# Halves of w_in and w_out stored to scratch in the second sub-block and loaded from there in the third and fourth

## The chip, the cores and the metric

The kernel runs on one core of one Trainium2 chip. The metric is the device time of one execution in microseconds (us), the median of several runs. The profile is one further execution, taken by the hardware profiler; its times count from the first instruction of the program.

## The reference

One inference step of one decoder layer. 2048 prompt tokens of one request and 32 decoding tokens (8 requests of 4) with 1024 features go through three sub-layers, each behind an RMS norm and with a residual add:

```
q, k, v, r, a, u, sv = split(rmsnorm(x) @ w_in)             # 256 256 512 512 16 512 512
o     = gated_linear_attention(q / 8, k, v, log_sigmoid(a @ w_alpha + b_alpha) / 16)
o     = rmsnorm(o) * silu(r)
s_out = gelu(u) * (tril(w_s) @ rmsnorm(gelu(sv)) + b_s)     # inside chunks of 128 tokens
h = x + concat(o, s_out) @ w_out                            # the mixer
h = h + softmax(rmsnorm(h) @ wq_x @ mk^T / 16) @ mv @ wo_x  # 256 memory tokens, 4 heads
h = h + (gelu(conv3(rmsnorm(h) @ w_gate)) * (rmsnorm(h) @ w_up)) @ w_down   # 2816 wide
y = rmsnorm(h)
```

w_in is 1024 x 2576, w_out 1024 x 1024; both are used for every token. Everything is fp32. Outputs are y for prompt and decoding tokens, the attention and convolution states, memory keys and values, and the decoding tokens' sv.

## The kernel before, in words

**Sub-blocks.** The prompt is cut into four sub-blocks of 512 tokens (s = 0 to 3), worked through one after the other: mixer, attention over the memory, feed-forward. The 32 decoding tokens ride along in the mixer of the second sub-block (`SAMPLE_MIX = 1`) and in the feed-forward of the third (`SAMPLE_FFN = 2`); their attention over their own caches is done beside the second sub-block's feed-forward. By the trace, the mixers' projections begin at about 73, 805, 1580 and 2250 us.

**Three products for one.** To keep fp32 precision, an operand is split into two parts of a faster type: `hi`, a rounded copy made by ACT (line 84), and `lo`, the rest, subtracted by DVE or POOL (line 85). `mm3` (lines 92 to 94) then multiplies hi by hi, hi by lo and lo by hi.

**Units of weights.** Weights come in units of 128 partitions by 1024 floats. `wload` (line 99) loads one on SP's queue into one of five raw buffers (`wraw`, names r_...), `wsplit` (line 105) splits it into one of five `whi` and one of five `wlo` buffers (h_..., l_...); `wunit` (line 112) does both. `wready` (line 118) instead loads two halves that already lie in DRAM scratch straight into a `whi` and a `wlo` buffer, with two loads on SP (line 124); the attention and the feed-forward from the second sub-block on work like that. `wkeep` (line 129) is `wunit` followed at once by two stores of the halves to scratch on SP (line 134); the first sub-block uses it for w_down. The other weights of the feed-forward are stored there too in the first sub-block, as parts and sums for a product scheme of seven instead of eight (lines 163 to 179), and the folded attention matrices are stored by `put` and `flush` (lines 288 to 294).

**Steps.** The program is a list of steps; a step has a function and the units that it needs. `run` (line 475) goes through the list in order and keeps the units `AHEAD = 5` in front of the steps:

```
for i, st in enumerate(steps):
    now[0] = i
    flush(i - 1)
    need += sum(cost(u) for u in st.units)
    while at < len(queue) and made < need + AHEAD:
        j, u = queue[at]
        ready.setdefault(j, []).append(u() if callable(u) else wunit(*u))
        made += cost(u)
        at += 1
    st.fn(*ready.pop(i, []))
```

`put` only notes a store together with the number of the step; `flush` issues it on ACT's queue once the program is two steps further, so that nothing waits on a fresh result. `weave` (line 457) mixes side steps into the main ones by their numbers. The framework sets all waits and, when the kernel is built, the order of the instructions on every engine from a simulated schedule; each engine and each queue then works in that fixed order, so a queue whose next transfer must wait holds up those behind it.

**The mixer.** `proj_steps` (line 780) makes 20 units of w_in per sub-block: `tm_steps` (line 677) for sv, v and r with tokens on the partitions, four units each, and `fm_step` (line 660) for k, q and two halves of u with features on the partitions, two units each. The 16 columns of a are held in SBUF throughout. `out_proj_steps` (line 1142) takes 8 units of w_out, first the four of the gating half, then the four of the attention half. Between them are woven the gated linear attention (`gla_steps`, line 892: seven levels of masked products, states and decay on DVE, ACT and POOL), the spatial gating (`sgu_steps`, whose `mix` makes z and its halves ch and cl), and the final norm and output of the sub-block before (`final_steps`, line 1566). All 28 units pass through `wunit` in each of the four sub-blocks. In the second, `smp` inside `gla_steps` loads the states of the decoding requests (sg, line 1068, on SP).

**The way into a sub-block.** `norm_in_steps` (line 697) loads x in four pieces of 128 tokens through four buffers on SP (line 708): two pieces first, two (`second`) once the first have been transposed, and, in the second sub-block, the decoding tokens. Then come the norm's statistics, a broadcast (bcp_x) and the split xh, xl, which the projection ws (sv) needs first. These steps are woven into the last w_down steps of the sub-block before (line 1654).

Of the kernel before, what the change touches and what calls it, by code (L numbers as in the profile page):

```python
# [9 lines left out]
F32 = mybir.dt.float32  # L10
F32R = mybir.dt.float32r
U8 = mybir.dt.uint8
AF = mybir.ActivationFunctionType
# [14 lines left out]
SAMPLE_MIX = 1  # L28
# [5 lines left out]
Q0, K0, V0, R0, A0, U0, SV0 = 0, 256, 512, 1024, 1536, 1552, 2064  # L34
# [3 lines left out]
def hymba_step_kernel(  # L38
# [9 lines left out]
    nc = tc.nc  # L48
    act, dve, pool, pe = nc.scalar, nc.vector, nc.gpsimd, nc.tensor
# [7 lines left out]
    dp = ctx.enter_context(tc.tile_pool(name="dp", bufs=1, space=DRAM))  # L57
# [54 lines left out]
    def wunit(*spec):  # L112
        return wsplit(wload(*spec), spec[-1])
# [4 lines left out]
    def wready(src, name):  # L118

        def load():  # L120
            out = []
            for x, tag in enumerate(("whi", "wlo")):
                t = wp.tile(list(src.shape[0:1]) + list(src.shape[2:]), F32R, tag=tag, name=f"{tag}_{name}")
                nc.sync.dma_start(t.bitcast(F32), src[:, x])
                out.append(t)
            return tuple(out)
        return load

    def wkeep(dst, *spec):

        def load():
            out = wunit(*spec)
            for x, t in enumerate(out):
                nc.sync.dma_start(dst[:, x], t.bitcast(F32))
            return out
        return load

# [147 lines left out]

    late, now = [], [0]

    def put(dst, src):
        late.append((now[0], dst, src))

    def flush(before=None):
        while late and (before is None or late[0][0] < before):
            _, dst, src = late.pop(0)
            nc.scalar.dma_start(dst, src)

    def rstd_of(out, ss, p, n, inv):
        t = narrow("rt")
# [51 lines left out]
    for l in range(7):  # L349
# [3 lines left out]
        v = mf[:, :64].rearrange("p (n h) -> p n h", h=half)  # L353
# [295 lines left out]
    def chunks_of(sample):  # L649
        return [(0, 272), (272, 272)] if sample else [(0, 512)]  # L650
# [6 lines left out]
            return hi, lo  # L657
        return load

    def fm_step(w, m0, get_xs, sample, evac, name, make=None):  # L660
# [12 lines left out]
        if make is not None:  # L673
            return Step(fn, [wmake(w, 4 * j, 4, m0, 256, f"{name}{j}", make, j) for j in range(2)])
        return Step(fn, [(w, 4 * j, 4, m0, 256, f"{name}{j}") for j in range(2)])

    def tm_steps(w, m0, get_xs, sample, evac, name):

        ps = {}

        def fn(j, wu):
            xs = get_xs()
            wh, wl = wu
            for c in range(5 if sample else 4):
                n = 128 if c < 4 else NS
                cs = slice(c * 128, c * 128 + n)
                if j == 0:
                    ps[c] = acc(f"t_{name}{c}") if c < 4 else mps(f"t_{name}{c}")
                for kk in range(2):
                    k = 2 * j + kk  # L690
                    mm3(ps[c][:n], xs[k][0][:, cs], xs[k][1][:, cs], wh[:, kk], wl[:, kk], k == 0, k == 7)
                if j == 3:
                    evac(ps[c][:n], c, n)
        return [Step(lambda wu, j=j: fn(j, wu), [(w, 2 * j, 2, m0, 512, f"{name}{j}")]) for j in range(4)]


    def norm_in_steps(B):
# [82 lines left out]
    def proj_steps(B):  # L780
        s, sample = B.s, B.mix_sample
        T = TM if sample else SB
        nt = 5 if sample else 4
        w = w_in[0]
        xs = lambda: B.xs

        def ev_tm(key, f):
            def evac(ps, c, n):
                if c == 0:
                    B.__dict__[key] = [U(f"{key}{s}{c}") for c in range(nt)]  # L790
                f(B.__dict__[key][c][:n, :512], ps)
# [23 lines left out]
        out = tm_steps(w, SV0, xs, sample, ev_tm("sv", gelu), f"ws{s}")  # L815
        out.append(Step(a_fn))
        out.append(fm_step(w, K0, xs, sample, ev_fm("k", 0, cpy), f"wk{s}"))
        out.append(fm_step(w, Q0, xs, sample,
                           ev_fm("q", 0, lambda o, i: act.activation(o, i, AF.Copy, scale=0.125)), f"wq{s}"))
        out += tm_steps(w, V0, xs, sample, ev_tm("v", cpy), f"wv{s}")  # L820
        out += [fm_step(w, U0 + h * 128, xs, sample, ev_fm("u", h, gelu), f"wu{s}{h}") for h in (0, 2)]
        out += tm_steps(w, R0, xs, sample, ev_tm("r", cpy), f"wr{s}")
        return out

    def norm_of(src, ss, c, n):
# [61 lines left out]
    for p in range(2):  # L887
        t = cp.tile([128, 128], F32, tag=f"S{p}", name=f"Sz{p}", bufs=2)
# [721 lines left out]
    for s in range(NSB):  # L1610
        B = NS_()
# [8 lines left out]
    after = []  # L1620
    for s, B in enumerate(blocks):
        proj = proj_steps(B)
        gla, gtail = gla_steps(B)
        sgu_st = sgu_steps(B)
        nst = len(sgu_st) - 4
        keep = None
        if B.mix_sample:
            def keep():
                if not hasattr(smp, "x"):
                    smp.x = U("smpx")  # L1630
                return smp.x
        w1, w2, stat = out_proj_steps(B, lambda k0, m2, s=s: (w_out[0], k0, 4, m2 * 256, 256, f"wo{s}{k0}{m2}"),
                                      lambda B=B: B.cat, "gx", "wo", B.mix_sample, 4, B.mix_sample, keep)
        folds = [(qk_steps, 0, 10), (vo_steps, 11, 19)] if s == 0 else []
        steps += weave(proj + w1, *folds, (after, 0, 5), (sgu_st[:nst], 11, 12), (sgu_st[nst:], 12, 17), (gla[:2], 5, 7), (gla[2:12], 8, 10), (gla[12:], 10, 13), (gtail, 16, 18))
        scales, sc, turns = attention_steps(B)
        x1, x2, xstat = out_proj_steps(B, lambda k0, m2, s=s: wready(vod[m2][k0 // 4], f"wx{s}{k0}{m2}"),
                                       lambda B=B: B.ao, "gffn", "wx", False, 0, B.ffn_sample, seven=s > 0, whole=True)
        steps += w2 + [stat, scales]
        steps += weave(sc + x1, (turns[:1], 1, 1), (turns[1:2], 2, 2), (turns[2:3], 3, 3), (turns[3:], 4, 4))  # L1640
        fin = final_steps(B)
        fstart, fmain, flast = ffn_steps(B, fin if s == NSB - 1 else None)
        steps += x2 + [xstat, fstart]
# [46 lines left out]
```

## Time and profile before

| | |
|---|---|
| median of 3 runs | 2920.62 us |
| the runs | 2920.65, 2915.56, 2920.62 us |
| the profiled execution | 2911.8 us |
| its span, first to last instruction | 2910.1 us |
| mean granted clock of TensorE | 0.993 |
| HBM read, written | 497.04 MB, 125.31 MB |
| DMA on SP's queue | 605.67 MB |

PE is TensorE's matmuls, PEld its weight loads, DVE, ACT and POOL the three other compute engines, SP the engine that issues most transfers; SPq marks its issuing. In rows of waits the numbers are microseconds in total, times, and the longest one. In rows that group instructions, the three numbers with slashes are the shortest, median and longest duration in ns. In rows by stretch of time, a busy time and a count stand for each engine, then the granted clock, the DMA engines' busy share and GB/s. In the chain a row has its start, its duration and what it is. In rows of the timeline the bracket holds the engine's idle time before the instruction and what ended it. Matmuls are pipelined, and their ends are modelled.

### The profile page before, as it was taken

How to read it: one execution, taken by the hardware profiler on the slowest of the kernel's cores; microseconds unless marked ns; L12 is line 12 of the kernel's file. 1: busy time of each engine (PE TensorE's matmuls, PEld its weight loads, DVE VectorE, ACT ScalarE, POOL GpSimd, SP SyncE). 2: the span in 40 equal slices, each digit the busy share in tenths (PEclk: the TensorE clock that was granted, in tenths of full speed). 3: DMA queues.
4: the chain of work that ended last, by engine and by line, in shares of the span. 5: the costliest groups of instructions: out<-in, count | busy, mean ns of one | idle time of the engine just before them, and what ended most of it. 6: DMA issues, size and time to landing. Idle time of an engine off the chain costs nothing.

```text
span 2910.1 us, 47402 instructions
## 1 busy us (share of the span) xinstructions
PE 2854.9 (98%) x18148; PEld 2524.1 (87%) x18148; DVE 1795.9 (62%) x3101; ACT 1049.8 (36%) x1904; POOL 672.1 (23%) x700
## 2 busy tenths in 40 slices
PE   8998999999999999999999999999999999999998
PEld 8887888888887799988888879899999788899998
DVE  7567558777647644645556674566666685465555
ACT  5635334333352423322223543422223544331221
POOL 1222213111122320222223231132222232132221
PEclk9999999999999999999999999999999999999999
DMA  9645679999932235877896214577776323577775
GB/s 310 198 149 182 209 227 334 333 336 333 334 101 66 68 103 187 291 279 246 309 327 235 87 59 136 189 253 260 250 266 232 106 67 101 183 260 256 278 278 180
DMA packets 360138, 625.49 MB, mean 215 GB/s; under 512 B 27195, under 2 KB 227838, under 8 KB 359912
## 3 DMA queue, kind: packets, MB, share of 16 engines
q1 hardware_dynamic: 346088, 605.67, 61.4%
q10 hardware_dynamic: 13824, 16.78, 1.6%
q8 instruction: 144, 2.36, 0.3%
q14 instruction: 82, 0.67, 0.1%
HBM read 497.04 MB, written 125.31 MB: 214 GB/s over the span
## 4 chain that ended last, share of the span: by engine, by line
PE 83%; DVE 3%; issue 1%; DMA 1%; ACT 1%; POOL 1%; DVEq 0%; POOLq 0%; SPq 0%; ACTq 0%
PE d L94 6%; PE d L92 6%; PE d L93 6%; PE sc L94 2%; PE sc L93 2%; PE sc L92 2%; PE a_wx L94 2%; PE a_wx L92 2%; PE a_wx L93 2%; PE a_wo L92 2%; PE a_wo L93 2%; PE a_wo L94 2%; PE a_wg L92 1%; PE a_wup L92 1%; PE a_wup L93 1%; PE a_wg L93 1%
## 5 line engine op out<-in xcount | busy, mean ns | idle before, releaser
L92 PE MATMUL d<-acth,whi_wd 128*128 128x512 f32 (+2 forms) x720 | 244.0, 339 | 0.0
L94 PE MATMUL d<-acth,wlo_wd 128*128 128x512 f32 (+2 forms) x720 | 242.8, 337 | 0.0
L93 PE MATMUL d<-actl,whi_wd 128*128 128x512 f32 (+2 forms) x720 | 242.3, 336 | 0.0
L1544 DVE TENSOR_TENSOR h<-d,h 128x512 f32<-128x512 f32 (+1 forms) x232 | 133.8, 582 | 156.0 <-PE d L94 155.7
L1483 POOL TENSOR_TENSOR c<-c,bc_f 128x512 f32<-128x512 f32 (+1 forms) x88 | 135.6, 1544 | 140.6 <-ACT c L1482 139.9
L94 PEld LDWEIGHTS d<-acth,wlo_wd 128*128 128x128 f32 x720 | 135.3, 188 | 15.5 <-issue 1.6
L92 PEld LDWEIGHTS d<-acth,whi_wd 128*128 128x128 f32 x720 | 135.4, 188 | 15.1 <-issue 1.6
L1473 ACT ACTIVATE c<-g,colsb 128x512 f32<-128x512 f32 x88 | 71.8, 816 | 211.8 <-DVE g L1442 158.1
L93 PEld LDWEIGHTS d<-actl,whi_wd 128*128 128x128 f32 x720 | 135.6, 188 | 13.6 <-issue 0.4
L92 PE MATMUL sc<-whi_qk,woh 128*128 128x256 f32 x512 | 144.4, 284 | 0.0
L94 PE MATMUL sc<-whi_qk,wol 128*128 128x256 f32 x512 | 144.3, 282 | 0.0
L93 PE MATMUL sc<-wlo_qk,woh 128*128 128x256 f32 x512 | 144.0, 283 | 0.0
L1505 POOL TENSOR_TENSOR c<-r_q_wup,c 128x512 f32<-128x512 f32 (+1 forms) x33 | 59.2, 1794 | 342.6 <-DVE r_q_wup L279 222.4
L1470 POOL COPY carry<-g 128x2 f32<-128x2 f32 x88 | 31.8, 361 | 428.6 <-DVE g L1442 426.5
L92 PE MATMUL a_wo<-ch,h_wo 128*128 128x512 f32 (+1 forms) x320 | 112.6, 359 | 8.7 <-ACT ch L84 7.1
L978 POOL TENSOR_TENSOR e<-e,k 128x512 f32<-128x512 f32 (+1 forms) x48 | 72.1, 1501 | 212.6 <-DVE kr L974 136.4
L93 PE MATMUL a_wo<-cl,h_wo 128*128 128x512 f32 (+1 forms) x320 | 114.2, 358 | 0.4 <-POOL cl L85 0.4
L94 PE MATMUL a_wo<-ch,l_wo 128*128 128x512 f32 (+1 forms) x320 | 113.9, 357 | 0.0
L1474 DVE SCALAR_TENSOR_TENSOR c<-g,colsb,c 128x512 f32<-128x512 f32 x88 | 86.1, 978 | 30.0 <-ACT c L1473 29.4
L92 PE MATMUL a_wx<-pTh,whi_wx 128*128 128x512 f32 x256 | 101.2, 395 | 0.0
L94 PE MATMUL a_wx<-pTh,wlo_wx 128*128 128x512 f32 x256 | 100.6, 393 | 0.0
L93 PE MATMUL a_wx<-pTl,whi_wx 128*128 128x512 f32 x256 | 100.5, 393 | 0.0
(3354 smaller groups left out, 9533.1 us busy)
## 6 DMA issues: line engine op xcount, KB each, us to landing
whi_wd<-wd SPq DMA_DIRECT2D x66, 512.0 KB
wlo_wd<-wd SPq DMA_DIRECT2D x66, 512.0 KB
r_wo<-in_w_out_dram SPq DMA_DIRECT2D x32, 512.0 KB
whi_qk<-qkd SPq DMA_DIRECT2D x32, 512.0 KB
wlo_qk<-qkd SPq DMA_DIRECT2D x32, 512.0 KB
wlo_wx<-vod SPq DMA_DIRECT2D x32, 512.0 KB
whi_wx<-vod SPq DMA_DIRECT2D x32, 512.0 KB
r_wg<-in_w_gate_dram SPq DMA_DIRECT2D x22, 512.0 KB
```

What stands on the lines that cost most here:

```text
L92: pe.matmul(ps, wh, xh, start=first, stop=False)
L93: pe.matmul(ps, wh, xl, start=False, stop=False)
L94: pe.matmul(ps, wl, xh, start=False, stop=last)
L978: pool.tensor_tensor(kl[:, :Tl], e[:, :Tl], B.k[p][:, :Tl], ALU.mult)
L1470: pool.tensor_copy(carry[:, f, :], g[:, SB:SB + 2])
L1473: act.activation(c[:, :SB], g[:, 2:SB + 2], AF.Identity, bias=cb, scale=w2)
L1474: dve.scalar_tensor_tensor(c[:, :SB], g[:, 1:SB + 1], w1, c[:, :SB], ALU.mult, ALU.add)
L1483: pool.tensor_tensor(c[:, :T], c[:, :T], B.fbc[:, :T], ALU.mult)
L1505: (dve, pool)[i].tensor_tensor(c[:, :T], q[i], c[:, :T], ALU.mult)
L1544: dve.tensor_tensor(B.h[m + mm][:, cs], ps[:, :cw], B.h[m + mm][:, cs], ALU.add)
```

## The change

The mixer's 28 units are made by a new function, `mixer_unit`, which goes by the sub-block. In the first it is as before. In the second, a unit is loaded and split as before, and the two halves are then noted with `put` for a store to a scratch tensor of their own, on SP's queue, issued two steps later. In the third and fourth, the halves are loaded from there with `wready`: no raw load, no split. `put` and `flush` get a queue for each store. `fm_step`, `tm_steps`, `proj_steps` and the call of `out_proj_steps` pass the function through.

```diff
+    mixd = {}
+
+    def mixer_unit(s, w, k0, nk, m0, mw, name):
+
+
+        key = name.split("_")[0], k0, m0
+        if s > SAMPLE_MIX:
+            return wready(mixd[key], name)
+        if s < SAMPLE_MIX:
+            return w, k0, nk, m0, mw, name
+        mixd[key] = dst = dp.tile([128, 2, nk, mw], F32, tag=f"mixd{len(mixd)}", name=f"mixd{len(mixd)}")
+
+        def load():
+            out = wunit(w, k0, nk, m0, mw, name)
+            for x, t in enumerate(out):
+                put(dst[:, x], t.bitcast(F32), nc.sync)
             return out
         return load
...
-    def put(dst, src):
-        late.append((now[0], dst, src))
+    def put(dst, src, queue=None):
+        late.append((now[0], dst, src, queue or nc.scalar))
 
     def flush(before=None):
         while late and (before is None or late[0][0] < before):
-            _, dst, src = late.pop(0)
-            nc.scalar.dma_start(dst, src)
+            _, dst, src, queue = late.pop(0)
+            queue.dma_start(dst, src)
...
-        return Step(fn, [(w, 4 * j, 4, m0, 256, f"{name}{j}") for j in range(2)])
...
+        return Step(fn, [unit(w, 4 * j, 4, m0, 256, f"{name}{j}") for j in range(2)])
...
-        return [Step(lambda wu, j=j: fn(j, wu), [(w, 2 * j, 2, m0, 512, f"{name}{j}")]) for j in range(4)]
+        return [Step(lambda wu, j=j: fn(j, wu), [unit(w, 2 * j, 2, m0, 512, f"{name}{j}")]) for j in range(4)]
...
+        def unit(*spec):
+            return mixer_unit(s, *spec[:-1], f"in_{spec[-1]}")
...
-        w1, w2, stat = out_proj_steps(B, lambda k0, m2, s=s: (w_out[0], k0, 4, m2 * 256, 256, f"wo{s}{k0}{m2}"),
+        w1, w2, stat = out_proj_steps(B, lambda k0, m2, s=s: mixer_unit(s, w_out[0], k0, 4, m2 * 256, 256, f"out_wo{s}{k0}{m2}"),
```

More of the change, by code (lines that the diff above doesn't have):

```diff
@@ L134, in load @@
                 nc.sync.dma_start(dst[:, x], t.bitcast(F32))
+            return out
+        return load
+    mixd = {}
[10 more added lines that the diff above has]
+                put(dst[:, x], t.bitcast(F32), nc.sync)
             return out
@@ L658, in wmake, with fm_step @@
         return load
-    def fm_step(w, m0, get_xs, sample, evac, name, make=None):
+    def fm_step(w, m0, get_xs, sample, evac, name, make=None, unit=lambda *spec: spec):
         def fn(*ws):
@@ L674, in fm_step, with tm_steps @@
             return Step(fn, [wmake(w, 4 * j, 4, m0, 256, f"{name}{j}", make, j) for j in range(2)])
[L675 to L677 removed]
+        return Step(fn, [unit(w, 4 * j, 4, m0, 256, f"{name}{j}") for j in range(2)])
+    def tm_steps(w, m0, get_xs, sample, evac, name, unit):
         ps = {}
@@ L813, in a_fn @@
                 dve.tensor_copy(B.aT[0:32, c0:c0 + cw], ps[:32, :cw])
-        out = tm_steps(w, SV0, xs, sample, ev_tm("sv", gelu), f"ws{s}")
+        def unit(*spec):
+            return mixer_unit(s, *spec[:-1], f"in_{spec[-1]}")
+        out = tm_steps(w, SV0, xs, sample, ev_tm("sv", gelu), f"ws{s}", unit)
         out.append(Step(a_fn))
[L817 to L822, printed above, removed]
+        out.append(fm_step(w, K0, xs, sample, ev_fm("k", 0, cpy), f"wk{s}", unit=unit))
+        out.append(fm_step(w, Q0, xs, sample, ev_fm("q", 0, lambda o, i: act.activation(o, i, AF.Copy, scale=0.125)),
+                           f"wq{s}", unit=unit))
+        out += tm_steps(w, V0, xs, sample, ev_tm("v", cpy), f"wv{s}", unit)
+        out += [fm_step(w, U0 + h * 128, xs, sample, ev_fm("u", h, gelu), f"wu{s}{h}", unit=unit) for h in (0, 2)]
+        out += tm_steps(w, R0, xs, sample, ev_tm("r", cpy), f"wr{s}", unit)
         return out
```

## The prediction

> **What bounds the kernel now.** I read the page's head first, then the busy time by stage, then, inside the stages that the change touches, the chain and the waits of TensorE.
>
> ```profile
> span 2910.1 us, 47402 instructions
> PE 2854.9 (98%) x18148; PEld 2524.1 (87%) x18148; DVE 1795.9 (62%) x3101; ACT 1049.8 (36%) x1904; POOL 672.1 (23%) x700
> ```
>
> TensorE is busy for 2854.9 of 2910.1 us, so at most 55 us of the span can be won without changing its work, and the change leaves every matmul as it is. Whatever it gives or costs must appear as TensorE waiting less or more. The next view cuts out the first feed-forward part (400 to 770 us) and the mixers of the second, third and fourth sub-block; its columns are busy time and instruction count of each engine, then the granted clock, the DMA share and GB/s.
>
> ```profile
> 400.00:770.00 370.00, 370.00 (x1613) 301.09 (x1612) 284.06 (x448) 150.28 (x200) 70.18 (x74) 1.00 1.02 327
> 812.00:1040.00 228.00, 216.08 (x1372) 182.04 (x1371) 133.33 (x287) 95.30 (x212) 62.77 (x44) 0.96 0.22 68
> 1575.00:1750.00 175.00, 170.84 (x907) 140.50 (x905) 125.47 (x221) 91.22 (x188) 56.57 (x39) 1.00 0.27 85
> 2262.00:2425.00 163.00, 158.93 (x855) 130.15 (x854) 117.66 (x212) 82.62 (x171) 47.41 (x34) 1.00 0.26 81
> ```
>
> Two things are to be seen. In the first row the DMA engines are full (share 1.02) with loads and stores of weight halves, all on SP's queue, and TensorE still never stops: 370.00 of 370.00. In the three mixers DMA is three quarters idle, TensorE loses 11.9, 4.2 and 4.1 us, and DVE (third number) is the next busiest engine, at 125.47 of 175 us in the third sub-block.
>
> **The change, part by part. Removed: the splits of the third and fourth sub-block.** A unit of weights is 128 partitions by 1024 floats, 0.524 MB; a mixer uses 20 units of w_in and 8 of w_out. Each is split by one ACT copy and one DVE subtraction:
>
> ```profile
> L84 ACT ACTIVATE h_ws<-r_ws x16: 1044/1060/1064, 52.6 to 2240.3; 128x1024 fp32r<-128x1024 f32 x16
> L85 DVE TENSOR_TENSOR l_ws<-r_ws,h_ws x16: 1212/1224/1227, 54.2 to 2241.4; 128x1024 fp32r<-128x1024 f32 x16
> ```
>
> So each of the two sub-blocks loses 28 x 1.06 = 29.7 us of ACT and 28 x 1.22 = 34.3 us of DVE. Nearly all of that lies beside matmuls. What lies on the chain that ended last is short; first the third sub-block, then the fourth (start, duration, what):
>
> ```profile
> 1576.35 1.21 DVE l_wk L85
> ...
> 1713.54 0.72 DVE l_wo L85
> ...
> 1717.97 1.13 DVE l_wo L85
> ```
>
> ```profile
> 2247.10 1.06 ACT h_wk L84
> ...
> 2261.95 1.05 ACT h_wk L84
> ...
> 2388.89 0.72 DVE l_wo L85
> ...
> 2393.32 1.14 DVE l_wo L85
> ```
>
> They sum to 1.21 + 0.72 + 1.13 = 3.06 us and 1.06 + 1.05 + 0.72 + 1.14 = 3.97 us, 7.0 us in all: the upper end of the gain. TensorE can only win back what it idles after those pieces. Its waits between 1560 and 1785 us, and then between 2225 and 2450 us:
>
> ```profile
> PE a_wo L92 <- ACT ch L84: 2.0, 1, 2.0
> PE s L985 <- POOL e L978: 0.7, 1, 0.7
> PE bcp_x L307 <- ACT h L730: 0.6, 1, 0.6
> PE t_ws L92 <- ACT xh L84: 0.4, 1, 0.4
> ```
>
> ```profile
> PE yp L1584 <- DVE y L1591: 0.9, 1, 0.9
> PE s L985 <- POOL e L978: 0.9, 1, 0.9
> PE t_ws L92 <- ACT xh L84: 0.8, 1, 0.8
> ```
>
> The first row, 2.0 us, is the last z of the spatial gating on its way to ch; no split stands in that chain, and it stays. The others sum to 1.7 and 2.6 us. I take 4.3 us, since TensorE is the bound and cannot gain what it does not idle; 0 and 7.0 us are the ends. Once those waits are gone, the 2.0 us of ch and the matmuls themselves are next.
>
> **Moved: where the halves of these two sub-blocks come from.** 28 units now bring 1.05 MB instead of 0.52, 14.7 MB more: over the 175 us of the third mixer 84 GB/s on top of 85, half of the 327 that the feed-forward part moved without a wait. A load into a split slot must wait for the matmuls five units back, and the lookahead of the five raw buffers is lost. The half that comes takes 1.05 MB / 327 GB/s = 3.2 us plus a latency below the 4.7 us of the x load shown further down; it is needed four units later, at 24 matmuls of 370/1613 = 0.229 us each, which is 22 us. Cost nothing, with 14 us of cover. SP issues 28 more loads in each of these mixers, a few tenths of a microsecond each (4 x loads took 2.04 us, below), some 14 us of SP in 175: nothing, unless something short stands behind them.
>
> **Added: 56 stores of 0.52 MB in the second sub-block, 29.4 MB.** Over 228 us that is 129 GB/s on top of 68, again far below 327. So the mean costs nothing; what counts is where single stores stand ahead of something urgent on SP's queue. The stores of a unit are queued two steps after its load, each waits on SP for its split, and all that SP has behind them waits too: loads of the next units, x, the states of the decoding requests. Two places are tight. The first is the sub-block's start, where the stores of the first sub-block's w_down units still run:
>
> ```profile
> 770.00:780.00 10.00, 10.00 (x45) 8.16 (x44) 5.78 (x7) 2.29 (x3) 0.00 (x0) 1.00 1.04 407
> 790.00:795.00 5.00, 5.00 (x30) 4.28 (x29) 4.20 (x7) 1.73 (x4) 0.00 (x0) 1.00 1.04 348
> 800.00:805.00 5.00, 2.98 (x18) 2.60 (x18) 3.83 (x18) 2.85 (x8) 0.54 (x1) 0.65 0.85 263
> ```
>
> ```profile
> 774.25 1.23 DVE L85 TENSOR_TENSOR l_ws<-r_ws,h_ws 128x1024 fp32r<-128x1024 f32 x1 [0.66 <-ACT h_ws L84]
> 779.35 1.22 DVE L85 TENSOR_TENSOR l_ws<-r_ws,h_ws 128x1024 fp32r<-128x1024 f32 x1 [0.21 <-ACT h_ws L84]
> 784.89 1.22 DVE L85 TENSOR_TENSOR l_ws<-r_ws,h_ws 128x1024 fp32r<-128x1024 f32 x1 [0.21 <-ACT h_ws L84]
> 791.00 1.22 DVE L85 TENSOR_TENSOR l_ws<-r_ws,h_ws 128x1024 fp32r<-128x1024 f32 x1
> ```
>
> ```profile
> 790.27 2.04 SPq L708 DMA_DIRECT2D x<-in_x_prompt_dram  x4
> ```
>
> ```profile
> 791.51 4.71 DMA x<-in_x_prompt_dram
> ```
>
> Up to 795 us the DMA engines are full, and TensorE then waits for the last x tiles: the 4.71 us load is on the chain, and from 800 to 805 us TensorE works 2.98 of 5 us. The first four units of this sub-block are split by 775.5, 780.6, 786.1 and 792.2 us, so the stores of up to three are ready before x is issued at 790.27. Each unit put ahead of x means 1.05 MB more before it, at 407 GB/s 2.6 us. The ends are nothing (x is queued first) and four units, 10.3 us. I take two, 5.2 us: the first two are ready ten microseconds ahead; the third, after its delay of two steps, may fall on either side.
>
> The Trainium skill bears on this: "DMA: Bandwidth & Descriptors", section "Queues, rings and completion order", says that on each DMA engine the descriptors of one issuing engine's ring are taken in ring order. By that rule a store that SP issues first goes first however urgent x is; by a free choice among waiting transfers the sum would drop to 1.6 - 4.3 = -2.7 us.
>
> The second place is the load of the decoding states, which the second sub-block makes once for each pair of heads and TensorE waits for; the rows are the first load's piece of the chain and the split that ends just before it.
>
> ```profile
> 931.80 5.32 DMA sg<-in_state_gla_dram
> ```
>
> ```profile
> 930.13 1.23 DVE L85 TENSOR_TENSOR l_wr<-r_wr,h_wr 128x1024 fp32r<-128x1024 f32 x1 [0.20 <-ACT h_wr L84]
> ```
>
> That split ends at 931.36, 0.4 us before sg is issued. A whole unit's stores ahead of both loads would cost 2 x 3.2 = 6.4 us, none would cost 0; I take one store ahead of one load, 0.52 MB / 327 GB/s = 1.6 us.
>
> **The sum.** -4.3 + 5.2 + 1.6 = +2.5 us. The profiled execution took 2911.8 us (span 2910.1 and 1.7 around it), so the sum against it is 2914.3; the three runs of before have their median at 2920.6, 8.8 above that execution, and there it is 2923.1 us. A measurement of this kernel can tell about 0.2%, 5.8 us, from no change.
>
> **The rivals.** *The stores find room* (25%): x and sg are queued ahead of the stores, and the whole 7.0 us on the chain come back: 2913.6 us. For it speaks the full DMA of 400 to 770 us beside a TensorE that never stops; against it, that in that stretch no short load was urgent, while x at 791 is.
>
> *The start of the second sub-block is held up* (27%), the case on the other side: the stores of all four first units stand ahead of x on SP, +10.3 us. The longer idle time also costs clock, as the profile shows around the first sg load, where TensorE idled 3.3 us of the ten:
>
> ```profile
> 912.00:933.00 21.00, 18.33 (x148) 16.65 (x146) 20.38 (x52) 3.47 (x7) 8.38 (x6) 1.00 0.17 52
> 933.00:943.00 10.00, 6.70 (x44) 4.59 (x44) 3.07 (x8) 0.44 (x1) 0.00 (x0) 0.66 0.34 104
> ```
>
> A mean of 0.66 over ten microseconds is 6.8 us at half rate; 3.3 of them were idle anyway, and in the other 3.5 half the work, 1.7 us, was lost. The 2.7 us of idling in the row before left the clock at 1.00. So -4.3 + 10.3 + 1.6 + 1.7 = +9.3, or 2929.9 us. It decides once more than two units go ahead of x. "TensorE: Matmul & The Clock Gate" in the Trainium skill, section "What's actually happening", has the same: after an idle window of about 3.4 us TensorE runs at half rate until it has been busy for as long; the trace agrees.
>
> *The weights come late* (6%): without the raw lookahead the first units of the third and of the fourth sub-block land after TensorE asks for them, a whole load of 5.3 us each, +10.6: 2933.7 us. Against it stand the 14 us of cover. That the change does not do what it says (splits that stay) I leave out: for those sub-blocks the code has no split left.
>
> **How the numbers follow.** The forecast's own case has 42%: 2923.1, from 2917 to 2927, as the second place costs 0 to 6.4 us and the gain is 0 to 7.0. All of the first rival lies beyond 5.8 us faster, so faster has 0.25; the held-up start and the late weights give slower 0.33; same has 0.42. Cases of both signs hold most of the chance, so the range for eight in ten goes from the first rival's 2913.6, less 2 for the runs' own scatter, to the held-up start's 2929.9 and half-way on to the late weights: 2911.5 to 2932.
>
> **What would show it.** Right: no h_ and l_ rows after 1540 us for the mixers' weights; DVE some 25 to 34 us lower than 125 in the third mixer; TensorE's waits there down to about 2 us; the last x load of the second sub-block landing some 5 us later than 796.2, with a longer wait of bcp_x or t_ws behind it. Wrong: an x load that still takes 4.7 us with stores before it, or TensorE waits on DMA whi_ in the third and fourth mixer.

## The result, and the profile after

The change makes the kernel slower: 2938.1 us (median of 5 runs, 2935.52 to 2943.55) against 2917.8 us for before beside it (5 runs, 2915.56 to 2920.65). That is +20.3 us, a ratio of 1.0070 with a 95% interval of 1.0054 to 1.0086. The prediction said 2923.1 us, +2.5, with 2932 as its upper bound.

The page's head, then the stretches (columns as before: busy time and count of PE, PEld, DVE, ACT, POOL, the granted clock, DMA share, GB/s):

```profile
span 2938.5 us, 47433 instructions
...
PE 2864.5 (97%) x18148; PEld 2530.4 (86%) x18148; DVE 1737.6 (59%) x3045; ACT 997.5 (34%) x1850; POOL 659.4 (22%) x700
```

```profile
790.00:795.00 5.00, 5.00 (x32) 4.31 (x31) 3.37 (x7) 1.67 (x3) 0.00 (x0) 1.00 1.05 402
800.00:805.00 5.00, 0.41 (x2) 0.01 (x1) 1.92 (x2) 1.15 (x2) 0.00 (x0) 0.86 1.05 393
810.00:815.00 5.00, 0.37 (x2) 0.00 (x0) 1.45 (x6) 0.78 (x3) 0.76 (x1) 0.84 0.93 305
...
1604.00:1774.00 170.00, 166.25 (x872) 136.86 (x873) 98.55 (x190) 64.36 (x152) 53.34 (x38) 1.00 0.43 146
```

The same 170 us of the third mixer in before, one row not shown yet:

```profile
1580.50:1750.20 169.70, 166.70 (x874) 137.27 (x875) 120.34 (x212) 87.33 (x178) 56.57 (x39) 1.00 0.25 80
```

The splits are gone as meant: DVE has 21.8 us less and ACT 23.0 less in the third mixer, DMA moves 146 instead of 80 GB/s. TensorE has as many matmuls as before and works 166.25 instead of 166.70 us there: nothing won in this stretch. Over the whole span TensorE is busy 9.6 us longer than before (2864.5 against 2854.9) with the same 18148 matmuls, and waits 18.8 us longer. At the start of the second sub-block, TensorE is nearly still from 800 to 805 us (0.41 us), and the DMA engines stay full (1.05), where before they had come down to 0.46 already from 795 us on:

```profile
795.00:800.00 5.00, 3.61 (x26) 3.03 (x24) 2.33 (x7) 4.53 (x12) 1.01 (x1) 1.00 0.46 150
```

Where the time went is read from the first matmuls of each part: when each group starts, against before. The columns are: all up to the transposes of x of the second sub-block, its start (xt to ws), its projections up to the decoding states, from there to the attention's first scores (sc), the start and mixer of the third and fourth sub-block, and all else.

| us over before | up to 2nd | start 2nd | projections | states to sc | start 3rd | mixer 3rd | start 4th | mixer 4th | else | sum |
|---|---|---|---|---|---|---|---|---|---|---|
| after | 3.7 | 10.1 | -2.2 | 7.8 | 3.8 | 0.5 | 5.2 | 0.2 | -0.7 | 28.4 |

The sum is that of two profiled executions. The one of before lies 6.0 us under its median (2911.8 against 2917.8), the one of after 2.1 over (2940.2 against 2938.1): 28.4 - 6.0 - 2.1 = 20.3. The 3.7 us of the first column are part of that scatter. They arise at 230 and 281 us, in the first sub-block, which the change leaves as it was: there TensorE's granted clock was 0.50 for 3.4 us each in the execution of after, and 1.00 in that of before. The -2.2 of the projections is scatter too: in before the clock was 0.50 from 859.5 to 862.9 us, and twelve of the 19 other executions profiled for this document show -1.8 to -2.3 there, among them the one that stores nothing and only loads the decoding states earlier (-1.9). In the mixers, too, such a dip comes and goes, so a column below some 3 us cannot be read from one pair of traces.

The chain that ended last names the late pieces (start, us, what):

```profile
788.09 10.40 DMA mixd<-l_in_ws
798.55 8.95 DMA x<-in_x_prompt_dram
...
808.94 6.24 DMA x<-in_x_sample_dram
...
944.99 7.29 DMA sg<-in_state_gla_dram
...
1589.05 4.88 DMA x<-in_x_prompt_dram
...
2264.29 6.26 DMA x<-in_x_prompt_dram
```

A store of weights, which nobody needs for 700 us, stands on the chain ahead of x; x then takes 8.95 us, before 4.71; sg takes 7.29, before 5.32. Of the 10.1 us of the second start, 7.3 are there at the last transposes of the prompt's x; 2.8 more come with the x of the decoding tokens (6.24 us; before, its first load took 1.75). Why a store delays a load that shares no data with it, SP's waits from 782 to 803 us show (waiter, what ended the wait, us in total, times, longest):

```profile
SPq L313 <- DMA wd<-l_wd: 2.8, 3, 1.1
SPq L727 <- DMA mixd<-l_in_ws: 1.9, 2, 0.9
...
SPq L102 <- DMA wd<-h_wd: 1.2, 2, 0.9
SPq L727 <- DMA r_in_wq<-in_w_in_dram: 1.0, 1, 1.0
SPq L102 <- DMA mixd<-l_in_ws: 0.9, 1, 0.9
```

and the same stretch of before:

```profile
SPq L708 <- PE xt L724: 6.4, 2, 3.8
SPq L102 <- DVE h L1544: 3.9, 1, 3.9
SPq L708 <- DMA x<-in_x_prompt_dram: 2.2, 1, 2.2
```

Before, SP waits mostly for buffers. After, the loads of x (L727) and of raw weights (L102) wait for the *end* of earlier transfers of other tensors. The trace shows why: each transfer issued by SP or ACT counts its end on one of eight counters (semaphores), taken in turn, and waits until the transfer that had the counter last, as a rule eight issues back, has ended. The last x load takes the counter of a load of r_in_wq issued at 789.19 us: that one ends at 799.90, and x is issued at 799.96. The transfers on SP's queue also land in the order in which they were issued, all 29 from 774 to 811 us. With the DMA engines full of half-megabyte pieces (0.524 MB at 402 GB/s is 1.3 us each), SP issues one piece per 1.3 us, and x goes out when its turn comes: the last x load at 799.96 us, before at 791.94 (3.7 of these 8.0 us are the scatter of the first column).

TensorE's waits from the decoding states on, then around the third and the fourth start:

```profile
PE ops L1102 <- DMA sg<-in_state_gla_dram: 13.0, 2, 6.9
...
PE bcp_x L326 <- DVE dg_x L325: 2.0, 1, 2.0
PE t_ws L92 <- ACT xh L84: 1.4, 1, 1.4
PE s L1007 <- POOL e L1000: 1.3, 1, 1.3
...
PE bcp_x L326 <- DVE dg_x L325: 2.1, 1, 2.1
...
PE t_ws L92 <- ACT xh L84: 1.5, 1, 1.5
PE s L1007 <- POOL e L1000: 1.4, 1, 1.4
```

and the first of these rows before:

```profile
PE ops L1080 <- DMA sg<-in_state_gla_dram: 4.3, 2, 3.3
```

13.0 us for sg instead of 4.3. The waits of bcp_x and t_ws, which were to end, are longer than before (0.6 and 0.4, and 0.8 for t_ws), as x comes late; the wait of s on e is longer too.

### The profile page after: what moved, and what is told of

Read it like the earlier page. It is cut to its first block, busy times and chain, and to the rows that moved or that the text cites. A ratio compares the mean times of both kernels' runs of the same rounds, so it can differ in the third digit from the quotient of the medians.

```text
span 2938.5 us, 47433 instructions
## 1 busy us (share of the span) xinstructions
PE 2864.5 (97%) x18148; PEld 2530.4 (86%) x18148; DVE 1737.6 (59%) x3045; ACT 997.5 (34%) x1850; POOL 659.4 (22%) x700
## 4 chain that ended last, share of the span: by engine, by line
PE 84%; DVE 2%; DMA 2%; ACT 1%; issue 1%; POOL 0%; SPq 0%; ACTq 0%; DVEq 0%; POOLq 0%
PE d L94 5%; PE d L92 5%; PE d L93 5%; PE sc L94 2%; PE a_wo L92 2%; PE sc L93 2%; PE sc L92 2%; PE a_wo L93 2%; PE a_wo L94 2%; PE a_wx L94 2%; PE a_wx L93 2%; PE a_wx L92 2%; PE a_wg L92 1%; PE a_wup L92 1%; PE a_wup L93 1%; PE a_wg L93 1%
## 5 line engine op out<-in xcount | busy, mean ns | idle before, releaser
L1000 POOL TENSOR_TENSOR e<-e,k 128x512 f32<-128x512 f32 (+1 forms) x48 | 65.8, 1371 | 214.3 <-DVE kr L996 181.5
L94 PEld LDWEIGHTS sc<-whi_qk,wol 128*128 128x128 f32 x512 | 96.9, 189 | 0.0
L92 PEld LDWEIGHTS sc<-whi_qk,woh 128*128 128x128 f32 x512 | 96.6, 189 | 0.1
L93 PEld LDWEIGHTS sc<-wlo_qk,woh 128*128 128x128 f32 x512 | 96.5, 189 | 0.2
```

The lines of the kernel that those rows point to most:

```text
L92: pe.matmul(ps, wh, xh, start=first, stop=False)
L93: pe.matmul(ps, wh, xl, start=False, stop=False)
L94: pe.matmul(ps, wl, xh, start=False, stop=last)
L1000: pool.tensor_tensor(kl[:, :Tl], e[:, :Tl], B.k[p][:, :Tl], ALU.mult)
```

## The experiments

Theory from these views: **short loads are late** (x at three starts, sg in the second mixer), because half-megabyte transfers are let out just ahead of them. Rivals: it is SP's order alone (another queue cures it); every megabyte costs, wherever it is. Each run is given with its difference from before on the same chip (medians) and the interval of the ratio.

**Stores alone** (third and fourth sub-block load and split as before).

```diff
-        if s > SAMPLE_MIX:
-            return wready(mixd[key], name)
-        if s < SAMPLE_MIX:
+        if s != SAMPLE_MIX:
             return w, k0, nk, m0, mw, name
```

> Leaves out the loads of stored halves: the third and fourth sub-block load raw and split as before; the stores of the second stay. Theory (stores stand ahead of x and of the decoding states on SP's queue, loaded halves stand ahead of x in the third and fourth): the second sub-block keeps its loss, about +15 us against before, and the third and fourth start as before, so +13 to +17 us in all. Rival (the halves loaded in the third and fourth cost most, through a later and larger load): under +8 us.

+13.4 us (1.0036 to 1.0069). Starts by the profile: +10.2 second, 0.0 third, 0.0 fourth; the states +6.2. Two thirds of the loss come with the stores; the rest, 6.9 us, with the loads. As a difference of medians from two chips these 6.9 are uncertain by nearly 7 us; the profiles show 9.0 at the two later starts.

**Without the six units of sv and k**, which are the first of each mixer.

```diff
+        if s < SAMPLE_MIX or key[0] == "in" and m0 in (SV0, K0):
+            return w, k0, nk, m0, mw, name
```

> The units of sv and k, the first six of each mixer, stay out of the change in all sub-blocks (raw load and split, no store); the other 22 are stored and loaded. Theory: with no store ahead of x at the start of the second sub-block and no doubled load ahead of x at the starts of the third and fourth, the +10 us and the two times +4 to +5 us go; left is the wait for the decoding states, +5 us, so +2 to +7 us against before. Rival (the cost comes from stored bytes and from the split's absence as a whole, wherever they are): 22/28 of it stays, +14 to +18 us.

+4.2 us (1.0011 to 1.0035), with 46.1 of the 58.7 MB still moved: starts -0.3, 0.0, 0.0, the states +5.1. So it is not the megabytes.

**Another queue for the stores, and another for the short loads.**

```diff
-                put(dst[:, x], t.bitcast(F32), nc.sync)
+                put(dst[:, x], t.bitcast(F32))
```

> The same stores, issued on ACT's queue instead of SP's. Theory of queue order: x and the decoding states no longer stand behind stores on SP; the second sub-block loses at most a third of its 15 us, and the total is +9 to +14 us (the third and fourth unchanged). Rival of bandwidth (the DMA engines are full, whichever queue the stores stand in): the last x load of the second sub-block still lands some 8 us late and the total stays at +17 to +22 us.

```diff
-                nc.sync.dma_start(t[:n, :512], src[:, j * 512:(j + 1) * 512])
+                (nc.scalar if s else nc.sync).dma_start(t[:n, :512], src[:, j * 512:(j + 1) * 512])
...
-                nc.sync.dma_start(t[:, :512].rearrange("p (b v) -> p b v", b=4), sgd[:, 4 * i:4 * i + 4, p])
+                nc.scalar.dma_start(t[:, :512].rearrange("p (b v) -> p b v", b=4), sgd[:, 4 * i:4 * i + 4, p])
```

> x from the second sub-block on, and the decoding states, are loaded on ACT's queue; stores and halves stay on SP. Theory of queue order: the short loads pass the half megabytes in all three sub-blocks, and nearly all is won back, 0 to +8 us against before. Rival of bandwidth: +15 us or more. A third outcome would be ACT held up by its own waits for x buffers: DVE and ACT later at the starts, over +8 us with x landing in 3 us or less.

Stores on ACT: +30.2 us (1.0091 to 1.0124), worse than the change and above both expectations. x and sg on ACT: +18.5 us (1.0047 to 1.0082), level with it. The second start loses 10.3 and 9.9 us. The x load on the chain, with the stores on ACT, then with x on ACT:

```profile
793.78 13.60 DMA x<-in_x_prompt_dram
```

```profile
798.55 6.67 DMA x<-in_x_prompt_dram
```

SP's order alone is not it. x on ACT's queue does pass transfers that SP had issued earlier: its first load, issued at 791.91 us, lands at 797.96, ahead of a raw load that SP had issued at 786.72 (798.48). Yet the last x still goes out only at 798.55 us, with the stores ahead of it on another queue; the eight counters are shared by both. Why the stores on ACT cost 10 us more than on SP is not resolved; TensorE then waits 15.2 us for sg instead of 13.0, and the states take 11.8 us instead of 7.8.

**The first units, stored but not loaded; and alone.**

```diff
+        if s < SAMPLE_MIX or s > SAMPLE_MIX and key[0] == "in" and m0 in (SV0, K0):
+            return w, k0, nk, m0, mw, name
```

> The six units of sv and k are stored in the second sub-block as in the change, but in the third and fourth their raw matrices are loaded and split as before; the other 22 units are as in the change. Theory (short urgent loads of x are late because half-megabyte transfers issued close to them fill the DMA engines): the starts of the third and fourth sub-block lose nothing (change: +3.7 and +5.3 us in the profile), the second still +8 to +11, the decoding states +4; in all +10 to +16 us over before. Rival (the traffic costs by the megabyte wherever it is): 52.4 of 58.7 MB are left, so +17 to +19 us.

```diff
+        if s < SAMPLE_MIX or not (key[0] == "in" and m0 in (SV0, K0)):
+            return w, k0, nk, m0, mw, name
```

> Only the six units of sv and k are stored and loaded again, the other 22 are as before. Theory of the late short loads: the starts of the second, third and fourth sub-block lose what they lose in the change (+8 to +11, +3.7, +5.3 us), the decoding states nothing: +12 to +19 us with 12.6 of 58.7 MB. Rival (by the megabyte): +4 us. Rival (the 22 other units take part in the starts): less than +8 us.

Stored, not loaded: +18.5 us (1.0044 to 1.0086), above the +10 to +16 that were forecast. By the profile the third and fourth start lose 0.1 and 0.8 us, as forecast, yet the median is only 2 us under the change: what the loads of these units cost lies between those 2 and the 8.1 us that the starts show. Alone: +17.7 us (1.0046 to 1.0085) with 12.6 of 58.7 MB; starts +9.4, +3.4, +4.6, the states +0.1. The rival by the megabyte (+4) is out.

**Half the stores.** Of the six units only the high halves are stored, and nothing is loaded from them.

```diff
-            for x, t in enumerate(out):
-                put(dst[:, x], t.bitcast(F32), nc.sync)
+            put(dst[:, 0], out[0].bitcast(F32), nc.sync)
```

> Of the six units of sv and k only the high halves are stored in the second sub-block (half the bytes and half the stores there), and nothing is loaded from them later; all else as before. Theory (the bytes ahead of the x loads on full DMA engines set the delay): the start of the second sub-block loses about half of the 9.4 to 10.1 us, 3 to 6 us, nothing else moves: +3 to +6 us. Rival (one store ahead of x is enough, by the order): +8 to +11 us. Rival (nothing is lost until the engines are full for longer): under +2 us.

+4.8 us (1.0012 to 1.0032); the start loses 4.3 us, close to half of 9.4. The loss goes with what is stored ahead of x; bytes and number of transfers were halved together, so which of the two counts is not separated.

**The counters, or the bandwidth?** x from GpSimd's queue, which has counters of its own; then the twelve stores from there.

```diff
-                nc.sync.dma_start(t[:n, :512], src[:, j * 512:(j + 1) * 512])
+                (nc.gpsimd if s else nc.sync).dma_start(t[:n, :512], src[:, j * 512:(j + 1) * 512])
```

> The change, with the loads of x issued from GpSimd's queue from the second sub-block on. In the built program each transfer issued from SP or ACT waits on one of eight counters taken in turn, shared by both, so it waits for the transfer eight issues before it; those from GpSimd have counters of their own. Theory of eight in flight: x is issued late because eight half-megabyte stores and loads are ahead of it whichever of the two queues it is on; from GpSimd the last x of the second sub-block goes out 6 to 8 us sooner against the change and the start loses 2 to 5 instead of 10 us: 4 to 9 us less than the change, +11 to +16 us over before. Rival (bandwidth alone: issued sooner, x still shares full engines): the start loses 8 us or more, +17 to +21 us. Third (GpSimd's own order holds x up): +20 us or more.

The rows of x around the second start:

```profile
L727 POOL DMA_DIRECT2D x<-in_x_prompt_dram x4: 536/536/627, 793.0 to 794.7; - x4
...
DMA to landing us min/median/max: 5.0/6.9/8.8
```

The last x goes out at 794.7 instead of 800.0 us and takes up to 8.8 us; the start loses 4.7 instead of 10.1. By this run about half of the loss is the wait to be issued, and half is sharing full engines. In all it is +22.8 us (1.0063 to 1.0094), no better than the change: the third and fourth start still lose 4.2 and 5.8 us. The sum is where the third expectation put it, but not for its reason, since x went out sooner.

```diff
-                put(dst[:, x], t.bitcast(F32), nc.sync)
+                put(dst[:, x], t.bitcast(F32), nc.gpsimd if key[0] == "in" and m0 in (SV0, K0) else nc.sync)
```

> The change, with the twelve stores of the sv and k units issued from GpSimd's queue, the rest as in the change. Theory of eight in flight: SP's loads no longer wait for these stores' ends, x goes out within 2 us of its time before and shares the engines with them only: the start of the second sub-block loses 3 to 6 instead of 10 us, +13 to +17 us over before. Rival (bandwidth alone): the start loses 8 us or more. Third (GpSimd's issuing delays its norm, gate and split work): the second sub-block loses more than in the change, +20 us or more.

+27.1 us (1.0073 to 1.0111), and the start loses 13.5: expectation missed. x goes out no sooner here, from 794.3 us on, and its first load holds SP for 5 us. What SP issues from 775 to 785 us takes 17 to 22 us to land, in the change some 10 to 11: with the stores on counters of their own more transfers are in flight at once, and each takes longer. The counters are therefore a part of the cause for x, but taking the stores out of them is no cure.

**The decoding states.** Their loads are issued with the first chunk of the attention's states instead of four steps later; first with the 22 units, then in before, then in the whole change.

```diff
-        def smp(p):
-            s0 = []
+        def smp_load(p):
+            B.sg = getattr(B, "sg", {})
+            B.sg[p] = []
...
-                s0.append(t)
+                B.sg[p].append(t)
+
+        def smp(p):
+            s0 = B.sg[p]
...
-            out += [lambda p=p, c=c: chunk(p, c) for c in range(4)]
+            out += [lambda p=p, c=c: (smp_load(p) if sample and c == 0 else None, chunk(p, c)) for c in range(4)]
```

> As the run without the sv and k units (+4.2 us over before), and the four loads of the decoding states are issued four steps earlier, with the first chunk, so six to ten places ahead on the SP queue. Theory: what was left of the loss is these loads' lateness: the waits of ops on sg (6.9 and 6.2 us in the change, 3.3 and 1.0 before) go to under 1 us each, and the time comes within 3 us of before, or under it since before waits there too. Rival (the loss there is TensorE waiting on something else, or the stores take it back later): still +3 to +6 us.

> The kernel before with only the four loads of the decoding states issued with the first chunk, four steps earlier; nothing is stored and loaded again. Theory: what made the run with early sg and 22 units faster than before (-6.7 us) is the early load alone, since before too waits 4.3 us for sg and then multiplies at a lower clock: -4 to -9 us. Rival (the stored units bring part of it through the splits that fall away): less than half of it, -3 to +1 us.

> The change whole, with only the four loads of the decoding states issued with the first chunk. Theory: the waits on sg (13.0 us) go, the three starts stay as late as in the change (+10, +3.7, +5.3 us): 10 to 15 us less than the change, so +5 to +10 us over before. Rival (the stores are only pushed to the next wait): within 4 us of the change, +16 to +20 us.

-6.7 us (0.9966 to 0.9988), -5.4 us (0.9973 to 0.9993) and +9.2 us (1.0025 to 1.0058). No wait on sg is left in any of them. The early load takes 5.4 us off before and 20.3 - 9.2 = 11.1 off the change: the change made this place 5.7 us worse. Joined from medians of three pairs, the 5.7 are uncertain by some 7 us; the profile's column says 7.8. TensorE's wait on sg is clearer: 11.6 to 15.2 us in the eight traces that store the units of r and load sg late, 3.5 to 4.3 in the five that load it late without such stores. A wait costs more than its length; the matmuls on sg before, after, and in before with early loads (shortest/median/longest ns):

```profile
L1080 PE MATMUL ops<-sg,qm x64: 270/273/423, 937.3 to 1008.3; 128*32 128x128 f32 x64
```

```profile
L1102 PE MATMUL ops<-sg,qm x64: 331/421/423, 952.4 to 1035.2; 128*32 128x128 f32 x64
```

```profile
L1084 PE MATMUL ops<-sg,qm x64: 272/273/297, 931.4 to 999.8; 128*32 128x128 f32 x64
```

After the waits of 6.9 and 6.2 us the median matmul takes 421 ns instead of 273. The granted clock is 0.50 from 946.9 to 960.6 and from 1022.0 to 1035.7 us, 13.7 us at each of the two waits; before, it was so for 6.8 and 3.4 us.

**All of it with both short loads helped**: x from GpSimd and sg early, both as above.

> The change whole, all 28 units, with x issued from GpSimd's queue and the loads of the decoding states issued with the first chunk. Theory: the two delays add and both go for the most part; from the change with early sg (+9 us over before) it takes 4 to 9 us off: 0 to +5 us. Rival (bandwidth alone): +7 to +11 us.

+3.7 us (1.0006 to 1.0028), inside the forecast, and 5.5 less than with early sg alone. Yet the two do not simply add up: x from GpSimd alone won nothing (+22.8 beside +20.3). Why it helps once sg is early is open; the 8 us by which the pair beats the sum of its parts are at the edge of what these medians can tell.

**What the splits are worth.** Ten units (q, v, u), none near a short load; the same with early sg; the same stored only; fourteen units (with r).

```diff
+        if s < SAMPLE_MIX or key[0] == "out" or m0 in (SV0, K0, R0):
+            return w, k0, nk, m0, mw, name
```

> Only the ten units of q, v and u are stored and loaded again: none is near the loads of x, and none is let out near the loads of the decoding states. Theory: nothing is late, and the splits that fall away were under no wait of TensorE that ends: within 3 us of before, no stage moved by over 1.5 us. Rival (by the megabyte, 21 of 58.7 MB): +7 us. Rival (the prediction's step of the gain: freed ACT, DVE and POOL let TensorE go on sooner): -1.5 to -4 us, in the third and fourth mixers.

> The ten units of q, v and u stored and loaded again, and the loads of the decoding states issued with the first chunk. Theory (the stored units cost and bring nothing where no short load is near them): within 3 us of before with early sg loads, so -4 to -9 us. Rival (the gain of the prediction shows once the other waits are gone): 2 to 4 us under before with early sg loads.

> The ten units of q, v and u stored in the second sub-block, but loaded raw and split in the third and fourth as before; the loads of the decoding states issued with the first chunk. Against it the run of the same ten units with their halves loaded (-10.6 us) differs by twenty splits. Rival (the loaded halves are worth something after all, as that run's lead of 5 us over before with early sg hints): -2 to -8 us, 3 us or more above it. Theory (they are worth nothing): -8 to -13 us, within 2 us of it.

> The fourteen units of q, v, u and r stored and loaded again, and the loads of the decoding states issued with the first chunk. Rival (loaded halves are worth about 0.25 us each, from 5 us for twenty splits): 1 to 3 us better than with ten units, -11 to -15 us. Theory (worth nothing, and the r stores are let out close to the second half of the sg loads): -4 to -10 us.

Ten units: -2.8 us (0.9984 to 1.0008), not told from none (in its profile the states take 3.7 us more than in before, with no longer wait on sg: 4.2 against 4.3). Ten with early sg: -10.6 us (0.9952 to 0.9978), beside -5.4 on the same chip with early sg alone. Ten stored only: -8.3 us (0.9955 to 0.9985). Fourteen, on the same chip as that: -14.1 us (0.9936 to 0.9964), 2904.15 us, the best of all and faster than both kernels. So the theory that the splits are worth nothing falls: with ten and with fourteen units loaded the kernel is 5.2 and 5.7 us faster than its neighbour without loaded halves. The intervals against before just overlap; the runs of each pair, taken against each other on their chip, differ in the mean by 5.1 and 4.8 us, with some 3 us either way at 95%. Between stored only and fourteen units, the third mixer differs by 3.6 us and the fourth by 2.5. TensorE's waits there, third and then fourth, stored only:

```profile
PE s L1005 <- POOL e L998: 1.8, 1, 1.8
...
PE s L1005 <- POOL e L998: 0.8, 1, 0.8
```

and all of its longer waits with fourteen units loaded:

```profile
PE a_wo L92 <- ACT ch L84: 2.0, 1, 2.0
PE bcp_x L326 <- ACT h L749: 0.7, 1, 0.7
PE t_ws L92 <- ACT xh L84: 0.4, 1, 0.4
PE yp L1610 <- ACT bc_x L328: 0.3, 1, 0.3
...
PE a_wo L92 <- ACT ch L84: 2.0, 1, 2.0
PE yp L1610 <- DVE y L1617: 1.0, 1, 1.0
PE t_ws L92 <- ACT xh L84: 0.8, 1, 0.8
```

The wait of s on e is gone in both, which is 1.8 and 0.8 us. The other 1.7 us or so of each mixer are one dip of the clock to 0.50 for 3.4 us, which stored only has and fourteen units have not. Whether the waits cause the dips is not shown: with stores alone the same waits (1.7 and 0.9) come without a dip. In the change it is there (1.3 and 1.4 us), and so it is, at 1.3 to 1.4 us, in the runs without sv and k, with and without early sg, which like the change load w_out. Without w_out's units it goes, with them it stays; why was not tried.

**The splits made twice**, in before.

```diff
-        return wsplit(wload(*spec), spec[-1])
+        raw = wload(*spec)
+        hi, lo = wsplit(raw, spec[-1])
+        if spec[-1][0] == "w" and spec[-1][1] in "skqvuro" and spec[-1][2] in "23":
+            split(hi, lo, raw)
+        return hi, lo
```

> The kernel before, with each of the 56 splits of w_in and w_out in the third and fourth sub-blocks made twice over (a second copy on ACT and a second subtraction on DVE of the same data): the suspected gain of the change with its sign turned, no traffic added. Theory (ACT's and DVE's time there is under no wait of TensorE that moves): within 4 us of before. Rival (the prediction's step: each unit's split time stands on the path at 4.3 us or more for all): +5 us or more, in the third and fourth mixers.

+42.3 us (1.0129 to 1.0169), with 15.4 and 15.3 us in the third and fourth mixer. (The names also took in eight units of the memory's keys and values at the program's head, where 8.8 us are lost by the second sub-block.) Of TensorE's waits in the third mixer, the longest that are new or longer than before:

```profile
PE a_wo L92 <- ACT ch L84: 3.2, 1, 3.2
...
PE t_wr L92 <- ACT u L807: 2.7, 1, 2.7
PE s L989 <- POOL e L982: 2.0, 1, 2.0
PE ktp L1028 <- POOL kh L1025: 1.5, 2, 0.8
```

The theory (within 4 us) is refuted: the mixer's side work has hardly any slack left. 28 splits more cost 15 us a mixer, of which three and four dips of the clock, as above, make up to 5.1 and 6.8; 14 fewer bring 0.8 to 1.8 in waits, and 28 fewer, in the change, nothing. The second split also lengthens each unit's own chain, so the two were not separated.

## Why the prediction was wrong

**The bound** holds: TensorE is busy for 2864.5 of 2938.5 us with unchanged matmuls, and what was lost is its waiting and its lower clock.

**The start of the second sub-block**, "I take two, 5.2 us", is the largest step that failed: it came to 10.1 us. The price of a unit was right, the count was not: seven stores, three and a half units, go out on SP from 782.53 to 797.22 us, ahead of the last x load. At 1.3 us each these are 9.1 us; the trace gives 7.3 up to the last transposes of the prompt's x. The other 2.8 come with the x of the decoding tokens, which has three more stores ahead of it and no term in the prediction. Half the stores gave 4.3 us. The upper end, four units and 10.3 us, was near in size and in count. The reason given, the order on SP's ring, is in the trace, where SP's transfers land in the order of their issue, but it is not the whole cause: x on ACT's queue passed transfers of SP and was as late as on SP's, and issued past the counters it still lost 4.7 us. "DMA: Bandwidth & Descriptors" in the Trainium skill, section "Issuing engines are not separate DMA queues", says that transfers started by different engines run on the same 16 DMA engines and interleave, and that using several saves only the time of issuing. The runs agree: +18.5 us with x on ACT beside +20.3.

**The decoding states**, "one store ahead of one load, 1.6 us", came to 5.7 us by the runs with early loads and 7.8 by the profile. Four stores go out just ahead of the first pair of loads (938.85 to 943.13 us) and six ahead of the second (1009.81 to 1016.65): both are late (TensorE waits 6.9 and 6.2 us), and the clock is 0.50 for 13.7 us at each. The upper end, 6.4, left out the clock.

**"Cost nothing, with 14 us of cover"** for the doubled loads was right for the weights: no wait of TensorE on whi_ or wlo_ halves appears. It was wrong for what stands behind them: x of the third and fourth sub-block lands late, 3.8 and 5.2 us at the two starts by the profile, 6.9 us for all loads by the medians. The prediction priced only the loads' own user. In the same way "SP issues 28 more loads ... nothing, unless something short stands behind them" named the condition and did not check that x meets it.

**The gain**, -4.3 us: in the change 0 (mixers +0.5 and +0.2), and the waits at the starts grew. One pair of traces could not tell this, but all of them can: with all 28 units loaded, seven traces have their two mixers 2.6 us above before on average, and the five traces with the mixers of before have 2.1. The mechanism itself exists: with ten or fourteen units it brought 5.2 and 5.7 us, near the 4.3 taken, though only 2.6 of the 5.7 are seen as waits. What failed is the step from freed waits to a gain of all 28 units.

**The sum** of the prediction with the measured terms: 0 + 10.1 + 5.7 + 6.9 = +22.7, beside the measured +20.3. That it comes so near is partly luck, as the last two terms are uncertain by some 7 us each. The rival that the start is held up (27%) had the main mechanism on the right side and still came out 8 us low (2929.9 against 2938.1), since it kept the gain and had no term for the other starts. Of the signs named, the splits' rows and DVE's time came as said (58.3 us less over both mixers); TensorE's waits there did not shrink to 2 us; the x load on the chain landed at 807.5 instead of 796.2, not 5 but 11 us later, 3.7 of them scatter.

## What to carry to other kernels

Spare bandwidth on the mean says nothing about a short load: ask which large transfers are let out just before it, count the stores that will be ready by then, and price them by their bytes over the full rate. A wait on a load needed at a known time was met best here by issuing it earlier, not by another queue: that alone made the kernel before 5.4 us faster. Leave out of such a scheme the units next to short loads; here fourteen of 28 units and early states give 2904.15 us.

## What was not expected

- A transfer from SP or ACT waits for the one that had its counter, as a rule eight issues before it, whatever the data and whichever of the two issues it: with full DMA engines SP issues one half-megabyte per 1.3 us, and a store of another tensor stands on the chain of x for 10.40 us.
- Moving stores off SP made it worse: +30.2 us on ACT's queue, +27.1 with twelve of them on GpSimd's, against +20.3.
- Two waits of 6 to 7 us raised the median of 64 matmuls from 273 to 421 ns, with the clock at 0.50 for 13.7 us at each wait.
- Profiled executions differ by 1 to 3 us in single stages with the same work, and most of it is the clock: a dip to 0.50 for 3.4 us, in which 1.7 us are lost, is there in one execution and absent in another, as in before at 859.5 us and after the change at 230 and 281 us. The third mixer took 2.4 us more with early sg loads alone than in before, with one such dip (1708.6 to 1712.0 us), so that 4 to 6 us of gain in two mixers could be told by medians beside each other and not from one pair of traces.
